# Passages between the parts of a float32 network on one core: program order written out, first products by token tile, norms on ScalarE and DVE

## The chip, the cores and the metric

The kernel runs on one core of a Trainium2 chip. TensorE (PE in the profile, its weight loads PEld) multiplies, VectorE (DVE), ScalarE (ACT) and GpSimd (POOL) do the rest, and SyncE (SP) issues the DMAs. The metric is the device time of one execution in microseconds; lower is better.

## The reference

Two blocks of a float32 network are applied to 256 tokens of 1024 channels. Each part adds its result to the residual x, and reads x through an RMS norm, `h = x * rsqrt(mean(x*x) + 1e-6) * g`, over the 1024 channels of a token:

```
x += (sigmoid(ga)*(attention @ w_a) + sigmoid(gb)*(gla @ w_b)) @ w_out     # mixer, 9 projections of h
a, u = split(h @ w_ffn_in); x += (silu(conv3(a)) * u) @ w_ffn_out          # FFN, 2816 wide
x += ((trailing_means(h) - h) @ w_pool per group of 256) * scale           # pool mixer
x += (silu(h @ w_gate) * (h @ w_up)) @ w_down                             # dense FFN, 2816 wide
x += ssd(h)                  # z, xbc, dt = h @ w_in; conv; chunked scan; gated norm; @ w_out
x += top 2 of 8 experts (3584 wide) by h @ w_router, weighted by their softmax
out = rmsnorm(x)
```

Each part needs the norm of the whole x of a token, that is the last sum of the part before it.

## The kernel before

**Tiles and stages.** The 256 tokens are two tiles of 128 on the partitions, t = 0 and 1; x stays in SBUF as two tiles of 128x1024, each in halves of 512 columns. The parts run one after the other (`network`, L1548). Every product of float32 matrices is made of three products of float32r parts, high by high, high by low and low by high (`mm3`, L337). Weights come by DMA on SP's queue into a ring of raw buffers (`fetch`, L287) of 128x2048; ScalarE copies the high part of each half of 1024 columns (`split`, L386: the copy is L391) and DVE subtracts it from the raw one to make the low part (L392). `piece` (L294) does that for one block of weights; there are six buffers for high halves (`wh`) and six for low halves (`wl`). In the experts the conversion is of 2048 columns at once (L311, L313).

**A norm** is `norm_tile` (L368): ScalarE squares both halves with a sum (L373), GpSimd multiplies the upper half by the gain (L374), DVE adds the two sums (L376), makes the reciprocal root by a shift, a constant and three rounds of tiny operations on 128x1 (`rsqrt`, L351 to L366), scales the lower half together with its gain (L378), and ScalarE scales the upper half (L379). Then `turn` (L398) transposes the tile's eight blocks by PE into two PSUM banks `tp` (L404) and splits them into the high and low part of xT (L391, L392). `Turned.tile` (L59) is the norm and the turn of one token tile.

**A passage** is what stands between the last products of one part and the first of the next: x of tile 0 is added (`add_x`, L429), normed and turned while tile 1's last products run, then the same of tile 1, then the first products of the next part for both tiles at once. There are three that the change touches: mixer to FFN (in `mixer`, L593), FFN through the pool mixer to the dense FFN (`down`, L778; `PoolMixer.tile`, L91), and dense FFN to SSD. In the pool mixer the trailing means are products with a band matrix, and the groups' outputs are products with w_pool. In both FFNs the first products are `sums` (L761): per block of 128 input channels and per bank, one matmul of 512 columns (both tiles, xT's high and low part by the high weights, L770) and one of 256 columns (L771); a chunk of weights is two banks of eight such pairs. In the SSD the first products are `z_chunk(0)` of 416 columns (`gemm_nat`, L409; `mm3`'s lines), for tile 0 and then for tile 1.

**What holds weights back and fills the waits.** After tile 1's turn `Turned.tile` sets `gates`: of the next pieces the first takes its low part on GpSimd, the next three wait with both their parts until the last split of xT has been issued (`piece`, L301 to L306). In the FFN and the dense FFN `keep_warm` (L328) puts 11 products whose results are not used ahead of tile 1's transposes; in the SSD none (the last argument of `Turned`, L1554 to L1556).

**Order.** The kernel is written with a planner that runs a timeline of its own when the program is built (`schedule_with_timeline_sim=True`, L1667) and fixes the order of the instructions on each engine: an operation that is ready by that timeline may be put ahead of one that stands earlier in the program. `issue_after` binds one instruction behind another. `in_order` (L1464) binds all instructions of PE, DVE and ACT issued from one point on in their program order, each engine for itself; others may still come between them. Before the change it is used in the experts. `Router` (L119) norms the input of the experts in its own way, with `rsqrt` in `scale` (L224).

## Time and profile before

| | |
|---|---|
| runs, us | 1767.45, 1766.4, 1769.3; median 1767.45 |
| the profiled execution, us | 1770.0; its span 1768.2 |
| PE busy | 1721.1 us, 97% of the span, 8731 matmuls |
| weight loads | 1420.7 us, 80% |
| DVE busy | 1495.5 us, 85%, 1652 instructions |
| ACT busy | 1245.7 us, 70%, 1412 instructions |
| GpSimd busy | 154.0 us, 9%, 118 instructions |
| DMA | 501.31 MB, mean 284 GB/s |
| chain that ended last | PE 55%, DVE 32%, issue 9% |

The span is the profiled execution on the core, from its first to its last recorded instruction. The granted clock of PE is given as a share of full speed, 2.4 GHz. A row of the timeline has the start, the duration, the engine, the line of the code, the operation, its result and its operands; in brackets is how long the engine was idle before it and what it waited for. Matmuls overlap their neighbours, so their pace is read from their starts. "x8" behind a row stands for eight instructions in a row.

### The profile page before, as it was taken

The numbers are of one execution on the slowest core, as the hardware profiler recorded it, in microseconds if no ns is written. First come the engines' busy times: TensorE is split into PE (matmuls) and PEld (weight loads), VectorE is DVE, ScalarE is ACT, GpSimd is POOL, SyncE is SP. The second block draws the span as 40 slices with busy tenths as digits, with TensorE's granted clock in tenths as the row PEclk, the third lists the DMA queues.
The fourth block names the chain that finished last, engine by engine and source line by source line (L and its number), as shares of the span: only waits on it lengthen the run. The fifth ranks groups of instructions, "written<-read, shape, count | busy, mean of one in ns | idle before, by whom it ended". The sixth has DMA issues, their size and how long they took to land.

```text
span 1768.2 us, 23830 instructions
## 1 busy us (share of the span) xinstructions
PE 1721.1 (97%) x8731; PEld 1420.7 (80%) x8731; DVE 1495.5 (85%) x1652; ACT 1245.7 (70%) x1412; POOL 154.0 (9%) x118
## 2 busy tenths in 40 slices
PE   8999989999999999999999999999999999999996
PEld 6878878888788879998878777777777787777775
DVE  7477668777766659997779999999999999999997
ACT  5564446655655546555468898888889888988895
POOL 1034010001100012572000000000000000000000
PEclk9999999999999999999989999999999999999999
DMA  8433455555455545425659999999999999999993
GB/s 288 167 120 123 143 183 211 185 188 188 143 188 188 188 150 204 143 97 179 253 187 373 420 421 421 420 418 420 405 402 420 421 420 415 421 420 410 421 420 157
DMA packets 72719, 501.31 MB, mean 284 GB/s; under 512 B 8322, under 2 KB 9346, under 8 KB 14355
## 3 DMA queue, kind: packets, MB, share of 16 engines
q1 hardware_dynamic: 72594, 499.71, 72.7%
q8 instruction: 71, 1.16, 0.3%
q14 instruction: 54, 0.43, 0.1%
HBM read 498.63 MB, written 1.05 MB: 283 GB/s over the span
## 4 chain that ended last, share of the span: by engine, by line
PE 55%; DVE 32%; issue 9%; ACT 2%; POOL 1%; DMA 0%; DVEq 0%; SPq 0%; ACTq 0%
DVE wl L313 23%; PE acc L339 7%; PE acc L340 7%; PE acc L341 7%; PE pr L770 5%; PE tp L770 5%; PE tp L771 2%; PE pr L771 2%; PE pr L339 2%; PE pr L340 2%; PE pr L341 2%; PE pr L1219 1%; PE pr L1218 1%; PE acc L516 1%; DVE wl L392 1%
## 5 line engine op out<-in xcount | busy, mean ns | idle before, releaser
L313 DVE TENSOR_TENSOR wl<-raw,wh 128x2048 fp32r<-128x2048 f32 x330 | 736.7, 2280 | 0.0
L311 ACT ACTIVATE wh<-raw 128x2048 fp32r<-128x2048 f32 x330 | 620.9, 1913 | 70.2 <-PE pr L341 38.8
L392 DVE TENSOR_TENSOR wl<-raw,wh 128x1024 fp32r<-128x1024 f32 (+2 forms) x248 | 308.2, 1255 | 112.7 <-ACT wh L391 109.8
L391 ACT ACTIVATE wh<-raw 128x1024 fp32r<-128x1024 f32 (+3 forms) x254 | 259.3, 1036 | 90.0 <-PE acc L341 60.1
L1219 PE MATMUL pr<-wl,xg 128*128 128x512 f32 x560 | 221.9, 396 | 5.5 <-DVE wl L313 5.5
L1218 PE MATMUL pr<-wh,xg 128*128 128x512 f32 x560 | 224.2, 400 | 0.0
L340 PE MATMUL pr<-wl,xg 128*128 128x512 f32 x336 | 135.8, 404 | 1.5 <-DVE wl L1462 1.5
L339 PE MATMUL pr<-wh,xg 128*128 128x512 f32 x336 | 136.6, 407 | 0.0
L341 PE MATMUL pr<-wh,xg 128*128 128x512 f32 x336 | 134.1, 399 | 0.0
L1219 PEld LDWEIGHTS pr<-wl,xg 128*128 128x128 f32 x560 | 105.3, 188 | 33.9 <-DVE wl L313 12.5
L770 PE MATMUL pr<-xT,wh 128*128 128x512 f32 x352 | 125.0, 398 | 2.0 <-DVE xT L392 2.0
L770 PE MATMUL tp<-xT,wh 128*128 128x512 f32 x352 | 124.9, 398 | 0.0
L1218 PEld LDWEIGHTS pr<-wh,xg 128*128 128x128 f32 x560 | 105.3, 188 | 22.2
L1219 PE MATMUL acc<-wl,hT 128*128 128x512 f32 x280 | 113.3, 405 | 1.6 <-DVE wl L313 0.4
L1218 PE MATMUL acc<-wh,hT 128*128 128x512 f32 x280 | 111.1, 397 | 0.7 <-DVE hT L392 0.7
L339 PE MATMUL acc<-wh,xT 128*128 128x512 f32 (+3 forms) x256 | 99.2, 389 | 1.6 <-ACT xT L391 0.9
L340 PE MATMUL acc<-wl,xT 128*128 128x512 f32 (+3 forms) x256 | 98.8, 387 | 0.0
L771 PE MATMUL tp<-xT,wl 128*128 128x256 f32 x352 | 98.6, 280 | 0.0
L771 PE MATMUL pr<-xT,wl 128*128 128x256 f32 x352 | 98.6, 280 | 0.0
L341 PE MATMUL acc<-wh,xT 128*128 128x512 f32 (+3 forms) x256 | 98.5, 387 | 0.1
L1536 POOL TENSOR_TENSOR raw<-x,raw 128x512 f32<-128x512 f32 x2 | 2.5, 1276 | 936.4 <-DVE x L431 936.4
L770 PEld LDWEIGHTS pr<-xT,wh 128*128 128x128 f32 x352 | 66.1, 188 | 18.4 <-DVE xT L392 2.4
(389 smaller groups left out, 3472.6 us busy)
## 6 DMA issues: line engine op xcount, KB each, us to landing
raw<-in_w_eg SPq DMA_DIRECT2D x110, 1024.0 KB, 10.6
raw<-in_w_ed SPq DMA_DIRECT2D x110, 1024.0 KB, 10.6
raw<-in_w_eu SPq DMA_DIRECT2D x110, 1024.0 KB, 10.8
raw<-in_w_ffn_in SPq DMA_DIRECT2D x22, 1024.0 KB, 4.9
raw<-in_w_dense_in SPq DMA_DIRECT2D x22, 1024.0 KB, 4.9
raw<-in_w_xbc SPq DMA_DIRECT2D x16, 1024.0 KB, 4.8
raw<-in_w_ffn_out SPq DMA_DIRECT2D x11, 1024.0 KB, 5.0
raw<-in_w_dense_out SPq DMA_DIRECT2D x11, 1024.0 KB, 4.9
```

The lines of the kernel that those rows point to most:

```text
L311: self.nc.scalar.activation(ab[0], raw, AF.Copy)
L313: lambda: v.tensor_tensor(ab[1], raw, ab[0].bitcast(F32), op=OP.subtract)
L339: mm(ps, st[0], mv[0], start=start, stop=False)
L340: mm(ps, st[0], mv[1], start=False, stop=False)
L341: self.last_mm = mm(ps, st[1], mv[0], start=False, stop=stop)
L391: a = nc.scalar.activation(h, src, AF.Copy)
L392: b = v.tensor_tensor(l, src, h.bitcast(F32), op=OP.subtract)
L516: nc.tensor.matmul(ps[:, m], wt.cut(a, k * 256 + m * P, P), xT[b][:, k], start=(k == 0 and a == 0 and b == 0), stop=(k == KB - 1 and b == 1))
L770: nc.tensor.matmul(ps, wh, xT[2][:, k], start=k == 0, stop=False)
L771: nc.tensor.matmul(ps[:, 0], wl, xT[0][:, k], start=False, stop=k == KB - 1)
L1218: self.nc.tensor.matmul(ps, st, mv[0], start=start, stop=False)
L1219: self.nc.tensor.matmul(ps, st, mv[1], start=False, stop=stop)
```

## The change

`Normed` replaces `norm_tile`. Its `half` squares one half of x on ScalarE, with a scale that makes the sum half of the mean, and multiplies the lower half by the gain on DVE; its `scale` makes the reciprocal root by `rsqrt_of` (the sum of both halves is taken in its first operation, and the constants differ), scales the lower half on ScalarE and the upper half with its gain on DVE. GpSimd has no part in it. The router's norm uses `rsqrt_of` too.

`Lead` holds the first weights of the next part: `fetch` reads them, `copy` and `subtract` make the parts of one half, `products` multiplies one half for one token tile. `LeadSums` does so for the first chunk of an FFN, with matmuls of 256 and 128 columns in place of 512 and 256, both banks of a tile for four blocks of channels at a time; `LeadRows` for the 416 columns of the SSD in four units, each per tile. `sums` and the SSD's first chunk use these results.

The instructions of each passage are issued in one written order, and `in_order` binds them: in the mixer from tile 0's last addition, ending with `both`; in the FFNs `down_last` takes the place of the last `down`: it fetches the next part's first weights, runs tile 0's last products, adds and norms tile 0, and within tile 1's last products calls `ready` (tile 0's turn, or its band products in the pool mixer, and the first weights' conversion), then `rest`. The pool mixer is cut into `means`, `split` and `mix` and its norm and that of the dense FFN are woven together. The `gates`, the products of `keep_warm` and GpSimd's low part of the first piece are gone.

```diff
+class Normed:
+    def __init__(self, net, g, xn):
+        self.net, self.g, self.xn = net, g, xn
+        self.ss = [net.small.tile([P, 2], F32, name="ss") for _ in range(2)]
+    def half(self, t, c):
+        net, nc, xn = self.net, self.net.nc, self.xn
+        h = slice(c * 512, (c + 1) * 512)
+        nc.scalar.activation(xn[:, t, 512:], net.x[:, t, h], AF.Square, scale=(0.5 / D) ** 0.5,
+                             accum_out=self.ss[t][:, c:c + 1])
+        if c == 0:
+            nc.vector.tensor_tensor(xn[:, t, h], net.x[:, t, h], self.g[:, h], op=OP.mult)
+    def scale(self, t):
+        net, nc, xn = self.net, self.net.nc, self.xn
+        r = net.rsqrt_of(self.ss[t], 1e-6)
+        nc.scalar.activation(xn[:, t, :512], xn[:, t, :512], AF.Copy, scale=r)
+        nc.vector.scalar_tensor_tensor(xn[:, t, 512:], net.x[:, t, 512:], r, self.g[:, 512:], op0=OP.mult, op1=OP.mult)
+class Turned(Normed):
+    def __init__(self, net, gname, lead=None):
+        super().__init__(net, net.gain(gname), net.norm.tile([P, 2, D], F32, name="xn"))
+        self.xT, self.lead = net.pair(KB), lead and lead(net)
+    def fetch(self):
+        self.lead.fetch()
+    def group(self, t, g, turned=None):
...
+        if turned is None:
+            turned = net.tp((P, 4, P))
+            for i in range(4):
+                nc.tensor.transpose(turned[:, i], self.xn[:, t, (4 * g + i) * P:(4 * g + i + 1) * P], net.ident)
+            return turned
+        last = net.split(turned, *[x[:, 4 * g:4 * g + 4, s] for x in self.xT[:2]])
+        if t == 0:
...
+    def turn(self, t):
+        for g in range(2):
+            self.group(t, g, self.group(t, g))
+    def ready(self):
+        self.turn(0)
+        self.lead.ready()
+    def rest(self):
+        lead, n = self.lead, self.lead.n
+        lead.subtract(n // 2)
+        self.scale(1)
+        for u in range(n // 2 + 1, n):
+            lead.subtract(u)
+        for u in range(n // 2 + 1):
+            lead.products(0, u, self.xT)
+        self.turn(1)
+        for u in range(n // 2 + 1, n):
+            lead.products(0, u, self.xT)
+        for u in range(n):
+            lead.products(1, u, self.xT)
+    def both(self):
+        ps = [self.group(0, g) for g in range(2)]
+        self.group(0, 0, ps[0])
+        net, s = self.net, slice(0, P)
+        net.nc.scalar.activation(self.xT[0][:, 4:, s], ps[1], AF.Copy)
+        self.scale(1)
+        self.early = net.nc.vector.tensor_tensor(self.xT[1][:, 4:, s], ps[1], self.xT[0][:, 4:, s].bitcast(F32), op=OP.subtract),
+        self.lead.products(0, 0, self.xT)
+        self.turn(1)
+        self.lead.products(0, 1, self.xT)
+        for h in range(2):
+            self.lead.products(1, h, self.xT)
+class Lead:
+    def __init__(self, net, aps, w):
+        self.net, self.aps, self.w = net, aps, w
+    def fetch(self):
+        raws = [self.net.fetch(ap, self.w) for ap in self.aps]
+        w = self.w // 2
+        self.raw = [raw[:, h * w:(h + 1) * w] for raw in raws for h in range(2)]
+        self.n, self.high, self.low = len(self.raw), {}, {}
+    def copy(self, u):
+        self.high[u] = self.net.whp.tile([P, 1024], F32R, name="wh")[:, :self.w // 2]
+        self.net.nc.scalar.activation(self.high[u], self.raw[u], AF.Copy)
+    def subtract(self, u):
+        self.low[u] = self.net.wlp.tile([P, 1024], F32R, name="wl")[:, :self.w // 2]
+        self.net.nc.vector.tensor_tensor(self.low[u], self.raw[u], self.high[u].bitcast(F32), op=OP.subtract)
+    def ready(self):
+        for u in range(self.n // 2):
+            self.copy(u)
+            self.subtract(u)
+        for u in range(self.n // 2, self.n):
+            self.copy(u)
+class LeadSums(Lead):
+    def products(self, t, h, xT):
+        net, mm = self.net, self.net.nc.tensor.matmul
+        if (t, h) == (0, 0):
+            self.ps = [net.pr((P, 2, T)) for _ in range(2)]
+        s = slice(t * P, (t + 1) * P)
+        for k in range(4 * h, 4 * h + 4):
+            for m in range(2):
+                c = slice(k % 4 * 256 + m * P, k % 4 * 256 + (m + 1) * P)
+                mm(self.ps[m][:, :, s], self.high[h][:, c], xT[2][:, k, :, s], start=k == 0, stop=False,
+                   skip_group_check=True)
+                mm(self.ps[m][:, 0, s], self.low[h][:, c], xT[0][:, k, s], start=False, stop=k == KB - 1,
+                   skip_group_check=True)
+class LeadRows(Lead):
+    def products(self, t, u, xT):
+        net, w = self.net, self.w // 4
+        if u == 0:
+            if t == 0:
+                self.ps = []
+            self.ps.append(net.acc())
+        s = slice(t * P, (t + 1) * P)
+        for i in range(2):
+            k, c = 2 * u + i, slice(i * w, (i + 1) * w)
+            net.mm3(self.ps[t][:, :w], (xT[0][:, k, s], xT[1][:, k, s]), (self.high[u][:, c], self.low[u][:, c]),
+                    k == 0, k == KB - 1)
+class PoolMixer(Normed):
...
+    def fetch(self):
+        self.N = self.then()
+        self.N.fetch()
+    def means(self, t, b, ps):
+        for g in range(2):
+            for i in range(4):
+                w, f = 2 * g + i // 2, slice((4 * g + i) * P, (4 * g + i + 1) * P)
+                c = slice(T, 3 * P) if b else slice(t * P, (t + 1) * P)
+                self.net.nc.tensor.matmul(ps[g][:, i], self.xn[:, b, f], self.band[:, w, c], start=b == 0 and i == 0,
+                                          stop=b == t and i == 3, skip_group_check=True)
...
+    def mix(self, t):
...
+        out = []
...
-            net.add_x(t, c, ps)
-        if t:
-            self.N.tile(1)
-            self.ctx.close()
+            out.append(ps)
+        return out
...
+    def ready(self):
+        ps = self.banks()
+        self.means(0, 0, ps)
+        self.split(0, ps)
+        self.N.lead.ready()
+    def rest(self):
+        net, N = self.net, self.N
+        N.lead.subtract(1)
+        self.scale(1)
+        out = self.mix(0)
+        ps = self.banks()
+        self.means(1, 0, ps)
+        for c in range(2):
+            net.add_x(0, c, out[c])
+            N.half(0, c)
+        self.means(1, 1, ps)
+        self.split(1, ps)
+        N.scale(0)
+        out = self.mix(1)
+        for c in range(2):
+            net.add_x(1, c, out[c])
+            N.half(1, c)
+        N.both()
+        self.ctx.close()
...
+        nc.scalar.activation(self.xh[:, t, h], x, AF.Square, scale=(0.5 / D) ** 0.5, accum_out=self.ss[:, t, c:c + 1])
...
+        self.r = net.rsqrt_of(self.ss[:, t], 1e-6)
...
-            gate = self.gates.pop(0) if self.gates else ()
...
+            fine = fine or self.wide is None
...
+    def rsqrt_of(self, ss, eps):
+        v = self.nc.vector
...
+        v.tensor_scalar(z, ss[:, 0:1], ss[:, 1:2], 0.5 * eps, op0=OP.add, op1=OP.add)
+        v.tensor_scalar(y.bitcast(I32), z.bitcast(I32), -0.5, float(0x5F3759DF - 0x400000 - 0x80000000), op0=OP.mult, op1=OP.add)
+        for _ in range(3):
+            v.tensor_scalar(t, y, y, z, op0=OP.mult, op1=OP.mult)
+            v.scalar_tensor_tensor(y, t, -1.5, y, op0=OP.add, op1=OP.mult)
+        return y
...
+            if then is not None and p == np_ - hold:
+                then.fetch()
+                for h in range(2):
+                    then.lead.copy(h)
+                    then.lead.subtract(h)
...
             def end(t, c, ps):
+                if (t, c) == (0, 1):
+                    self.start = len(nc.cur_bb.bb.instructions)
...
-                if c:
-                    N.tile(t)
-            for c in range(2):
-                self.gemm_nat(mT, I["w_out"][c], KB, end, c, last=True)
+                N.half(t, c)
+                if (t, c) == (0, 1):
+                    N.scale(0)
+            self.gemm_nat(mT, I["w_out"][0], KB, end, 0, last=True)
+            self.gemm_nat(mT, I["w_out"][1], KB, end, 1, last=True, then=N)
+            N.both()
+            self.in_order(self.start)
...
+        wt = None if lead else self.piece(ap)
...
+            ps = lead.ps[m] if lead else bank((P, 2, T))
+            for k in range(0 if lead else KB):
...
+    def down_last(self, aps, hT, accs, N):
+        wts = [self.piece(ap) for ap in aps]
+        N.fetch()
+        def sums(t, c, j):
+            for i in range(2):
+                h = hT[2 * j + i]
+                s = slice(t * P, (t + 1) * P)
+                self.mm3(accs[t][c], (h[0][:, s], h[1][:, s]), wts[j].both(i * 1024 + c * 512, 512), False,
+                         i == 1 and j == len(aps) - 1)
+        for j in range(len(aps)):
+            for c in range(2):
+                sums(0, c, j)
+        begin = len(self.nc.cur_bb.bb.instructions)
+        for c in range(2):
+            self.add_x(0, c, accs[0][c])
+            N.half(0, c)
+        N.scale(0)
+        for c in range(2):
+            for j in range(len(aps)):
+                if (c, j) == (1, 1):
+                    N.ready()
+                sums(1, c, j)
+            self.add_x(1, c, accs[1][c])
+            N.half(1, c)
+        N.rest()
+        self.in_order(begin)
...
+                a, u = self.sums(w_in[m], xT, self.tp if m % 2 else self.pr, pool, None if m else N.lead)
...
-            self.down([w_out[i + j] for j in range(3)], hs[2 * i:], accs, False, self.add_x, then=N)
+            self.down_last([w_out[i + j] for j in range(3)], hs[2 * i:], accs, N)
...
+                self.gemm_nat(xT, ap[max(c - 2, 0)], KB, gate_z, c, w=w, bank=bank)
...
-            z_chunk(0)
+            for t in range(2):
+                gate_z(t, 0, N.lead.ps[t][:, :416])
...
-            N.tile(t)
-        n.gates = []
-        N = n.mixer(N, lambda: Turned(n, "ln_ffn", 11))
-        M = n.ffn(N, I["w_ffn_in"], I["w_ffn_out"], True, lambda: PoolMixer(n, lambda: Turned(n, "dense", 11)))
-        N = n.ffn(M.N, I["w_dense_in"], I["w_dense_out"], False, lambda: Turned(n, "ssd", 0))
+            for c in range(2):
+                N.half(t, c)
+            N.scale(t)
+            N.turn(t)
+        sums = lambda w: lambda net: LeadSums(net, [w[0]], 2048)
+        N = n.mixer(N, lambda: Turned(n, "ln_ffn", sums(I["w_ffn_in"])))
+        M = n.ffn(N, I["w_ffn_in"], I["w_ffn_out"], True, lambda: PoolMixer(n, lambda: Turned(n, "dense", sums(I["w_dense_in"]))))
+        N = n.ffn(M.N, I["w_dense_in"], I["w_dense_out"], False,
+                  lambda: Turned(n, "ssd", lambda net: LeadRows(net, [I["w_z0"][0][0], I["w_z0"][0][1]], 1664)))
```

## Rows read from the trace of the kernel before

**Rows 1.** Windows: stretch, length, busy PE, PEld, DVE, ACT, POOL, clock, DMA, GB/s.
```profile
12.00:24.00 12.00, 10.34 (x41) 7.37 (x42) 11.60 (x23) 8.81 (x16) 3.83 (x2) 0.81 0.77 276
251.30:264.65 13.35, 10.65 (x60) 8.65 (x59) 10.89 (x20) 8.62 (x13) 1.28 (x1) 1.00 0.23 68
443.60:470.26 26.66, 22.96 (x156) 20.04 (x155) 21.39 (x48) 15.06 (x28) 6.44 (x5) 1.00 0.26 83
475.00:630.00 155.00, 155.00 (x829) 132.75 (x828) 99.67 (x138) 85.78 (x138) 0.00 (x0) 1.00 0.55 188
648.40:664.40 16.00, 13.49 (x67) 11.94 (x66) 11.53 (x20) 10.30 (x15) 3.09 (x2) 0.89 0.60 210
654.80:658.10 3.30, 3.30 (x12) 2.81 (x13) 1.38 (x2) 1.98 (x4) 0.00 (x0) 0.51 0.07 15
910.00:1700.00 790.00, 780.24 (x3490) 612.35 (x3490) 773.00 (x485) 685.31 (x523) 0.00 (x0) 1.00 1.01 413
```

**Rows 2.** Timeline of the first passage, all engines: start us, us, engine, line, operation.
```profile
251.31 1.03 PE L404 MATMUL tp<-ident,xn 128*128 128x128 f32 x8
251.51 0.69 DVE L431 TENSOR_TENSOR x<-x,acc 128x512 f32<-128x512 f32 x1 [0.69 <-PE acc L341]
...
252.44 0.62 ACT L373 ACTIVATE xn<-x 128x512 f32<-128x512 f32 x1
...
252.96 0.19 ACT L373 ACTIVATION_READ_ACCUMULATOR xn<-x 128x1 f32 x1
...
253.32 2.79 PE L335 MATMUL tp<-xT 128*128 128x512 f32 x11 [0.98 <-DVE xT L392]
...
258.15 1.29 DVE L392 TENSOR_TENSOR xT<-tp,xT 128x512 fp32r<-128x512 f32 x2 [1.44 <-ACT xT L391]
...
258.90 0.50 PE L770 MATMUL pr<-xT,wh 128*128 128x512 f32 x1 [0.98 <-DVE xT L392]
...
264.65 0.40 PE L770 MATMUL tp<-xT,wh 128*128 128x512 f32 x1
```

**Rows 3.** Timeline of PE in the second passage.
```profile
459.20 2.79 PE L335 MATMUL tp<-xT 128*128 128x512 f32 x11 [0.98 <-DVE xT L392]
...
470.26 0.39 PE L770 MATMUL tp<-xT,wh 128*128 128x512 f32 x1
```

**Rows 4.** Timeline of DVE at the start and before the first passage.
```profile
8.15 1.80 DVE L378 SCALAR_TENSOR_TENSOR xn<-x,rs_y,gbc 128x512 f32<-128x512 f32 x1 [1.07 <-DMA gbc<-in_gains]
...
16.16 0.14 DVE L376 TENSOR_TENSOR ss<-ss 128x1 f32<-128x1 f32 x1
...
17.06 1.22 DVE L392 TENSOR_TENSOR wl<-raw,wh 128x1024 fp32r<-128x1024 f32 x1
...
19.16 1.21 DVE L392 TENSOR_TENSOR wl<-raw,wh 128x1024 fp32r<-128x1024 f32 x1
...
21.29 0.75 DVE L378 SCALAR_TENSOR_TENSOR xn<-x,rs_y,gbc 128x512 f32<-128x512 f32 x1
...
247.61 0.54 DVE L376 TENSOR_TENSOR ss<-ss 128x1 f32<-128x1 f32 x1 [0.85 <-ACT xn L373]
...
250.07 0.75 DVE L378 SCALAR_TENSOR_TENSOR xn<-x,rs_y,gbc 128x512 f32<-128x512 f32 x1
```

**Rows 5.** Groups by line and shape, up to 920 us: busy us, mean ns | idle before, releaser.
```profile
L391 ACT ACTIVATE xT<-tp 128x512 fp32r<-128x512 f32 x20 | 11.5, 594 | 11.0 <-PE tp L404 11.0
...
L173 DVE TENSOR_TENSOR xs<-x,g 128x512 f32<-128x512 f32 x4 | 2.7, 688 | 0.0
```

**Rows 6.** Timeline of PE in the third passage.
```profile
654.79 1.90 PE L404 MATMUL tp<-ident,xn 128*128 128x128 f32 x8 [2.18 <-DVE xn L378]
...
664.20 0.35 PE L341 MATMUL acc<-wh,xT 128*128 128x416 f32 x1
664.39 0.28 PE L757 MATMUL acc<-xT,wl 128*128 128x256 f32 x1
664.51 0.28 PE L758 MATMUL acc<-xT,wh 128*128 128x256 f32 x1
```

More of the change, by code (lines that the diff above doesn't have):

```diff
@@ L47, in both @@
         return self.cut(0, a, w), self.cut(1, a, w)
-class Turned:
-    def __init__(self, net, gname, warm=0):
-        self.warm = warm
-        self.net, self.g = net, net.gain(gname)
-        self.xn = net.norm.tile([P, 2, D], F32, name="xn")
-        self.xT = net.pair(KB)
-    def tile(self, t):
-        self.net.norm_tile(t, self.g, self.xn)
-        if t and self.warm:
-            self.net.keep_warm(self.xT[0][:, 0, :P], self.xT[0][:, :4, :P], (self.net.turned, self.net.last_mm), self.warm)
-        last = self.net.turn(self.xn, KB, self.xT, ts=(t,))
-        if t:
-            self.net.gates = [(None,)] + [last] * 3
-        else:
-            self.early = last
@@ L73, in __init__ @@
     def __init__(self, net, then):
-        self.net, self.then, self.N = net, then, None
+        self.then, self.N = then, None
         I = net.I
@@ L81, in __init__ @@
         self.sc = net.gain("pool_scale", pool.tile([P, D], F32, name="sc"))
-        self.g = net.gain("pool", pool.tile([P, D], F32, name="g"))
-        self.xn = pool.tile([P, 2, D], F32, name="xn")
+        super().__init__(net, net.gain("pool", pool.tile([P, D], F32, name="g")), pool.tile([P, 2, D], F32, name="xn"))
         raw = net.fetch(I["w_pool"])
@@ L89, in __init__, with split @@
         self.wt = net.piece(Loaded(raw), pool=pool)
-    def tile(self, t):
-        net, nc, pT, xn, band = self.net, self.net.nc, self.pT, self.xn, self.band
-        net.norm_tile(t, self.g, xn)
-        s = slice(t * P, (t + 1) * P)
-        for g in range(0, 4, 2):
-            ps = net.tp((P, 4, P))
-            for i in range(4):
-                w, f = g + i // 2, slice((2 * g + i) * P, (2 * g + i + 1) * P)
-                nc.tensor.matmul(ps[:, i], xn[:, 0, f], band[:, w, s], start=True, stop=t == 0)
-                if t:
-                    nc.tensor.matmul(ps[:, i], xn[:, 1, f], band[:, w, T:], start=False, stop=True)
-            net.split(ps, pT[0][:, 2 * g:2 * g + 4, s], pT[1][:, 2 * g:2 * g + 4, s])
-        if t:
-            self.N = self.then()
-            self.N.tile(0)
+    def fetch(self):
[8 more added lines that the diff above has]
+                                          stop=b == t and i == 3, skip_group_check=True)
+    def split(self, t, ps):
+        s = slice(t * P, (t + 1) * P)
+        for g in range(2):
+            self.net.split(ps[g], *[p[:, 4 * g:4 * g + 4, s] for p in self.pT[:2]])
+    def mix(self, t):
+        net, pT = self.net, self.pT
+        s = slice(t * P, (t + 1) * P)
+        out = []
         for c in range(2):
@@ L249, in __init__ @@
         self.acts = pool("acts", 1)
[L250 removed]
+        self.ctx, self.rings, self.raws, self.nraw = ctx, rings, [], 0
         self.raw = self.more_raw(0, side="left")
@@ L407, in turn, with gemm_nat @@
         return last
-    def gemm_nat(self, xT, aps, kb, done, c, w=512, last=False, bank=None):
+    def gemm_nat(self, xT, aps, kb, done, c, w=512, last=False, bank=None, then=None):
         ps = [(bank or self.acc)() for _ in range(2)]
@@ L759, in pair_gemm, with sums @@
         return ps
-    def sums(self, ap, xT, bank, pool):
+    def sums(self, ap, xT, bank, pool, lead=None):
         nc = self.nc
-        wt = self.piece(ap)
+        wt = None if lead else self.piece(ap)
         out = []
         for m in range(2):
-            ps = bank((P, 2, T))
-            for k in range(KB):
+            ps = lead.ps[m] if lead else bank((P, 2, T))
+            for k in range(0 if lead else KB):
                 wh, wl = wt.both(k * 256 + m * P, P)
```

36 lines of the change are left out of this document (8 added, 28 removed).

## The prediction

> **What bounds the kernel now.** The stage windows come first. In the dense FFN the TensorE (PE) is busy for all 155.0 of 155.0 us; in the mixture of experts PE, DVE and DMA are all near full, the DMA at 413 GB/s [rows 1]. A stage of the first kind hands on an earlier or later start to the microsecond; the last one starts its stream of weights when its buffers come free, so it moves as a whole. What the change can win or lose is therefore what it wins or loses in the passages between parts, plus something at the start. The reader is to see in the windows how little that is. The first passage runs from PE's last product of w_out to the end of the first 256 columns of w_ffn_in, 251.30 to 264.65 us: 13.35 us, of which 2.70 idle and 2.79 filled by 11 warming products [rows 1, 2]. The second, FFN through pool mixer to dense FFN, 443.60 to 470.26, has 3.70 idle and the same filling again [rows 1, 3]. The third, dense FFN to SSD, 648.40 to about 664.3, has 2.51 idle and 3.30 us at a granted clock of 0.51, which is 1.2 of 2.4 GHz and costs 1.65 [rows 1]. Together 16 us lie open, 0.9% of the time.
>
> Then the timeline of one passage shows the order of waits: x is added (251.51), squared on ScalarE (252.44, readable at 253.15), a chain of tiny DVE operations makes the reciprocal root, xn is scaled, turned, copied, its low part taken, and PE starts at 258.90 [rows 2]. One norm chain undisturbed takes 2.46 us, of which 0.54 is the sum that the change drops [rows 4]; I take 1.95 for the new one and 0.72 for the scaling behind it (0.75 less what overlaps).
>
> **The change, part by part.** I lay the new program order out as one list per engine, each instruction starting when its engine and its inputs are there. Prices: adding x 0.66, a low part of xT 0.65 (two take 1.29), a Square readable 0.72 after it starts [rows 2]; a copy of xT 0.59 (0.5 where another follows), the product with the gain, now on DVE, 0.69 [rows 5]; a low part of 1024 weights 1.22 (1.18 in a row) [rows 4].
>
> *Split products.* A pair of matmuls of 512 and 256 columns costs 0.36 us now: 16 pairs fill 258.90 to 264.65 [rows 2]. By tiles it is 256 and 128 columns, twice. 256 columns follow each other at 0.12 [rows 6]; 128 columns I take at 0.11, as eight transposes of that width take 1.03 us with the drain of the last in it [rows 2] (bounds 0.06, half of 0.12, and 0.13, an eighth of 1.03). So 0.23 per pair and tile, 1.84 for half a chunk of one tile, 7.36 for all where 5.75 stood: 1.6 us more PE work in each of the first two passages.
>
> A rule of the skill speaks against this split. The Trainium skill, "TensorE: Matmul & The Clock Gate", section "LDWEIGHTS (loading the stationary operand)", gives a weight load as its columns over 1.2 GHz, 107 ns for 128, so that halving the moving columns below 256 saves hardly anything; the transposes agree with it. The same page's section "Back-to-back issue gap" has 81 ns per matmul sustained at 128 columns, by which a chunk would cost 6.4 us and the sum below would be 1.9 lower (an estimate); the transposes here are slower than that.
>
> *First passage.* DVE sets it. From 251.31: 0.2 to the end of the matmul, add 0.66, then 1.43 of waiting, since ScalarE's copy of xT now stands behind the Square (0.08+0.72+0.5+0.13), low part 0.65, norm 2.67, low part 0.65: 257.57. PE: the last four transposes to 258.09 (they waited for the PSUM bank of that low part), then three half chunks, 5.52: 263.61 against 264.65, so -1.0. The half that moved ahead is hidden by the norm of tile 1.
>
> *Second passage.* The band products of tile 0 go in among the last FFN products, which so end at 445.1 (16 passes of 0.11 later). From there, on DVE: wait 0.27, add 0.66, low weights 1.18, norm 2.67, add, gain, add 2.0, waiting behind two Squares 1.43, two low parts 1.3, norm 2.67, add, gain, add 2.0, waiting 1.43, low part 0.65, norm 2.67, low part 0.65. That is 19.6, so 464.7; PE +0.5 +5.5 gives 470.7 against 470.26 [rows 3]: +0.5. The early band products help nothing, because DVE is the chain and takes its operations in one fixed order.
>
> *Third passage.* Tile 0's turn goes in among tile 1's FFN products; its FFN products end at 640.1 (36 of 0.23 before the window's start) and its norm by the same list at 644.4. From there DVE has: add and gain 1.34, waiting 1.0, two low parts 1.3, two low parts of w_z0 1.96 (half of the four were GpSimd's; 1.2 by 832 of 1024 columns, 0.98 each), add 0.66, low weights 0.98, norm 2.67: 654.4. Tile 1's turn starts about where it does now, 654.79 [rows 6]. But then only the turn, 0.9, and five of eight units of 6 x 0.19 remain, 5.7: 661.1 against 664.3 [rows 6], -3.2.
>
> *The rest.* One DVE operation less in the router's chain: -0.2. At the start the scaling waits for the gain's DMA at 8.15 in either order [rows 4]; DVE takes over 0.69 per tile and loses contention and a tiny operation: 0, bounds -2 and +1. SP's queue keeps its order: gain and first weights of the next part are fetched into the same ring behind the same buffers. The removed GpSimd products lay off the path.
>
> At full clock and with nothing put between, the sum is -1.0+0.5-3.2-0.2 = -3.9.
>
> *Two costs on top.* (a) The clock. After 2.18 us without a product in the third passage the granted clock was 0.51 for 3.3 us [rows 1, 6]. My lists leave PE idle for 2.1 us in the first passage, 2.0 and 3.2 in the second, 1.7 in the third, the warming products being gone. A fall costs up to 1.65, less where PE waits anyway. I take 0.4, 0.6 and 0.7; bounds 0 and 5. (b) The gates that held back the weights of the next chunks are gone, and only the passage's own instructions are tied to each other. At the start, where no gates stood, two weight subtractions got into one chain: 5.13 us instead of 2.46 [rows 4]. Four such subtractions of 1.18 are ready in each of the first two passages (six buffers, raw weights there), two in the third. Each put in as soon as it is ready, they delay the three passages by 1.5, 3.5 and 2.4 in my lists: 7.4 at most, 0 at least. I take two that count, 2.4: the chains of this trace stand nearer to the clean end, the ungated one at the other.
>
> Sum: -3.9+1.7+2.4 = +0.2 on the profiled execution's 1770.0 (span 1768.2). That one lies 2.5 above the median of the runs, 1767.45; so 1767.7.
>
> **The rivals.**
> - *Weights get between* (slower). All ready subtractions go into the norm chains. Place: the norm of tile 1 in each passage, worst in the pool mixer, where DVE has no slack. Price: -3.9+1.7+7.4 = +5.2, 1772.7. It decides slower when more than 5.7 of the 7.4 are paid. For it: the start's chain. Against: DVE waits 1.43 three times, which swallows as many.
> - *Overlap as meant* (faster). Nothing gets between and the clock holds, as it does now over waits of about 1 us; the start gains a little, since GpSimd no longer slows DVE: a scaling took 1.80 beside GpSimd at 8.15 against 0.75 alone [rows 4], with DVE 97% busy and PE idle for 1.66 of 12 us there [rows 1]. -3.9-1 = -4.9: 1762.5. Against: the waits of 2 us above.
> - *No effect*: what it moves was hidden and the passages end where they did, 1767.5.
>
> On the second the Trainium skill, "SBUF — State Buffer", has the rule that a DVE operation with two SBUF inputs and a GpSimd one exclude each other on the shared port pair; the 1.80 agrees, and no number here hangs on it.
>
> **How the numbers follow.** A measurement of this kernel tells about 0.2%, 3.5 us, from no change. Forecast, some insertions and some falls of the clock: 0.45, own range 1764.5 to 1770.5. Overlap as meant: 0.27. Weights between: 0.25. No effect: 0.03. Nearly all of the overlap's lies beyond -3.5 (0.26) and most of the weights' beyond +3.5 (0.24), the rest within: 0.50. The hand-laid lists and the start are uncertain by 2.5 us together, so the range reaches that far past the two outer cases, 1762.5 and 1772.7: 1760 to 1775, one in ten left out on either side.
>
> **What would show it.** Right: the second passage no shorter than 26.7 us, counted from the last FFN product less the band products among them; the third about 3 shorter; a granted clock near 0.5 behind some of the idle stretches; weight subtractions of the next chunk between the tiny operations of a chain. Wrong: chains of 2 us with nothing between, a granted clock of 1.00 throughout, or a second passage below 26 us; then DVE is not its chain, and the change is faster than I say.

## The result, and the profile after

The changed kernel takes 1780.89 us (1780.25 to 1781.74), the kernel before in the same runs 1768.38: a ratio of 1.0071, 95% interval 1.0059 to 1.0084, so slower by 12.5 us. The forecast was 1767.7, the range 1760 to 1775. The profiled execution took 1780.25 us, its span is 10.2 longer than that of before; before's own execution lay 1.6 above its median and this one 0.6 below, which is the rest.

The head of the page, with the clock's row, of the kernel after:

```profile
span 1778.4 us, 23884 instructions
PE 1723.4 (97%) x8773; PEld 1427.7 (80%) x8773; DVE 1503.7 (85%) x1656; ACT 1246.9 (70%) x1412; POOL 127.1 (7%) x102
PEclk8999989999899999999989999999999999999999
```

Shares of busy time say nothing here: 97% as before. The clock's row has an 8 in the first, the sixth and the eleventh of the 40 slices, where before it has nines. The first is the start, where all kernels below but e3 have it; the others, 222 to 267 and 445 to 489 us, hold the first two passages. The windows of the kernel after (stretch, length, busy us of PE, PEld, DVE, ACT, POOL, clock, DMA share, GB/s) answer to [rows 1]: first the three passages, from the last product of the part before, then the stretches in them at half clock.

```profile
250.86:267.46 16.60, 12.55 (x83) 11.77 (x81) 9.63 (x22) 6.63 (x11) 0.00 (x0) 0.79 0.45 159
447.52:478.59 31.07, 23.75 (x163) 23.02 (x161) 22.23 (x47) 13.96 (x26) 0.00 (x0) 0.84 0.33 124
658.41:676.00 17.59, 13.12 (x65) 11.84 (x64) 13.11 (x22) 10.82 (x16) 0.00 (x0) 0.90 0.55 199
254.70:261.50 6.80, 6.05 (x28) 5.65 (x28) 4.03 (x12) 2.53 (x5) 0.00 (x0) 0.50 0.57 209
456.00:462.80 6.80, 5.85 (x27) 5.79 (x27) 4.77 (x11) 3.25 (x7) 0.00 (x0) 0.50 0.47 183
469.70:473.10 3.40, 3.40 (x19) 3.40 (x18) 2.04 (x7) 1.32 (x2) 0.00 (x0) 0.50 0.22 86
667.70:671.10 3.40, 3.40 (x14) 3.29 (x13) 3.40 (x5) 1.20 (x2) 0.00 (x0) 0.50 0.58 166
```

Where [rows 1] had the first passage at 13.35 us with 2.70 idle, it is now 16.60 with 4.05 idle and 6.8 us at half clock; the second had 26.66 with 3.70 idle, now 31.07 with 7.3 idle and 10.2 us at half clock. These windows begin at the start of the last product, 0.23 us earlier than those of [rows 1], and the second no longer holds tile 0's 16 band products, about 2 us, which now stand ahead of it.

Why PE idles stands in DVE's timeline (start, duration, engine, line, operation). In the first passage, the norm of tile 0, line by line from the first tiny operation to the scaling:

```profile
247.38 0.21 DVE L526 TENSOR_SCALAR rs_x<-ss 128x1 f32<-128x1 f32 x1 [0.85 <-ACT xn L60]
247.63 0.15 DVE L527 TENSOR_SCALAR rs_y<-rs_x 128x1 int32<-128x1 int32 x1
247.82 0.27 DVE L529 TENSOR_SCALAR rs_t<-rs_y,rs_x 128x1 f32<-128x1 f32 x1
248.13 0.16 DVE L530 SCALAR_TENSOR_TENSOR rs_y<-rs_t,rs_y 128x1 f32<-128x1 f32 x1
248.34 1.23 DVE L544 TENSOR_TENSOR wl<-raw,wh 128x1024 fp32r<-128x1024 f32 x1
249.48 0.27 DVE L529 TENSOR_SCALAR rs_t<-rs_y,rs_x 128x1 f32<-128x1 f32 x1
249.66 1.23 DVE L544 TENSOR_TENSOR wl<-raw,wh 128x1024 fp32r<-128x1024 f32 x1
250.81 0.15 DVE L530 SCALAR_TENSOR_TENSOR rs_y<-rs_t,rs_y 128x1 f32<-128x1 f32 x1
251.07 1.23 DVE L544 TENSOR_TENSOR wl<-raw,wh 128x1024 fp32r<-128x1024 f32 x1
252.21 0.27 DVE L529 TENSOR_SCALAR rs_t<-rs_y,rs_x 128x1 f32<-128x1 f32 x1
252.43 1.23 DVE L544 TENSOR_TENSOR wl<-raw,wh 128x1024 fp32r<-128x1024 f32 x1
253.58 0.15 DVE L530 SCALAR_TENSOR_TENSOR rs_y<-rs_t,rs_y 128x1 f32<-128x1 f32 x1
253.76 0.75 DVE L69 SCALAR_TENSOR_TENSOR xn<-x,rs_y,gbc 128x512 f32<-128x512 f32 x1
```

Four subtractions of the next chunks' weights stand one behind each of four tiny operations: the chain takes 6.38 us to the scaling, where tile 1's in the same trace takes 1.94 alone. The written order binds the chain's own operations to each other; the weights' are not among them.

In the second passage ScalarE is the first to be late. Its timeline, from the first weights' copies to tile 1's last Square:

```profile
445.69 2.00 ACT L149 ACTIVATE wh<-raw 128x1024 fp32r<-128x1024 f32 x2
447.58 3.88 ACT L543 ACTIVATE wh<-raw 128x1024 fp32r<-128x1024 f32 x4
451.37 0.61 ACT L60 ACTIVATE xn<-x 128x512 f32<-128x512 f32 x1
451.89 0.19 ACT L60 ACTIVATION_READ_ACCUMULATOR xn<-x 128x1 f32 x1
```

x was complete at 448.64 (the addition at 447.95 below); the Square waits for the last four of the six copies, those of the next chunks, and its sum is there at 452.08. DVE meanwhile takes the four subtractions and begins the norm when they are done, another 2.15 us later:

```profile
447.95 0.69 DVE L588 TENSOR_TENSOR x<-x,acc 128x512 f32<-128x512 f32 x1
...
449.69 4.62 DVE L544 TENSOR_TENSOR wl<-raw,wh 128x1024 fp32r<-128x1024 f32 x4
454.23 0.20 DVE L526 TENSOR_SCALAR rs_x<-ss 128x1 f32<-128x1 f32 x1
```

In the third passage ScalarE has the same, and a thing that I had not on my lists, the Exp of the SSD's decay (L1089) with its table load:

```profile
657.14 1.68 ACT L149 ACTIVATE wh<-raw 128x832 fp32r<-128x832 f32 x2
658.84 1.28 ACT L1089 ACT_TABLE_LOAD   x1
660.13 0.23 ACT L1089 ACTIVATE ea<-rows 128x32 f32<-128x32 f32 x1
660.27 1.67 ACT L149 ACTIVATE wh<-raw 128x832 fp32r<-128x832 f32 x2
661.85 1.99 ACT L543 ACTIVATE wh<-raw 128x1024 fp32r<-128x1024 f32 x2
663.74 0.61 ACT L60 ACTIVATE xn<-x 128x512 f32<-128x512 f32 x1
```

x was complete at 660.63, the Square starts at 663.74. Behind tile 1's scaling DVE then takes three subtractions of weights, two of them of the next chunks (667.10 to 670.30), before the low parts of xT.

To compare kernels whose order differs I take marks that stand behind each passage: the start of DVE's ninth `hl` subtraction of the FFN (319.15 us before) and of the dense FFN (524.04), from which on a kernel's distance to before stays the same through the rest of the FFN, the last product with w_xbc (788.66), the first of the experts (897.97), the end. Differences to the kernel before in each stretch between marks, in us, from the traces' timelines; the start is the first addition to x. "Chunk" is the distance from one `hl` subtraction to the next in the FFN and in the dense FFN, the last column the time at half clock in each of the three passages, by the records of the clock:

| kernel | start | 1st passage | 2nd | 3rd | router | experts | chunk, FFN and dense | half clock in 1st, 2nd, 3rd |
|---|---|---|---|---|---|---|---|---|
| before | | | | | | | 5.65, 5.55 | 0, 0, 3.4 |
| after | -0.2 | +2.3 | +7.0 | +2.0 | -1.2 | +0.2 | 5.55, 5.65 | 6.8, 10.2, 3.4 |
| e2 warm, no gates | +0.6 | +2.9 | +5.7 | +1.7 | -2.1 | -0.1 | 5.65, 5.65 | 3.4, 0, 0 |
| e3 before, no gates | +0.2 | +6.5 | +11.1 | +5.8 | -1.9 | -0.4 | 5.65, 5.65 | 6.8, 13.7, 6.8 |
| e4 before, no warm | -1.7 | +0.9 | +2.4 | 0.0 | -2.0 | -0.7 | 5.55, 5.55 | 6.8, 6.8, 3.4 |
| e5 gates, Exp misplaced | -0.2 | -0.5 | +6.0 | -2.5 | -0.2 | +0.1 | 5.65, 5.65 | 3.4, 10.2, 0 |
| e6 norms alone | -0.8 | -0.3 | -0.1 | -1.7 | -1.1 | 0.0 | 5.65, 5.65 | 0, 0, 0 |
| e7 gates, Exp | -2.0 | -1.1 | +3.4 | -2.5 | -1.9 | -0.4 | 5.55, 5.65 | 3.4, 6.8, 0 |
| e8 gates, Exp, warm | -1.6 | -1.9 | +0.5 | -2.6 | -1.2 | -0.4 | 5.55, 5.55 | 0, 0, 0 |
| e9 gates, planner's order | -1.1 | -1.8 | +2.4 | -1.2 | -1.2 | -0.1 | 5.65, 5.65 | 0, 6.8, 0 |
| e10 gates on DVE alone | +1.7 | -0.9 | +3.6 | +1.7 | -0.2 | -1.0 | 5.55, 5.55 | 3.4, 3.4, 6.8 |
| e11 Exp alone | +0.4 | +2.4 | +7.1 | +0.2 | -2.1 | -0.1 | 5.55, 5.65 | 6.8, 10.2, 0 |
| e12 no order, no gates | +0.6 | +2.8 | +3.1 | +2.9 | -1.2 | 0.0 | 5.55, 5.55 | 6.8, 3.4, 6.8 |

Two things limit what a row says. The chunks behind a passage follow at 5.55 or at 5.65 us, by the time of the mark a difference of 0.7, for a reason that I did not find; I name it where it counts, as "pace". And a trace is one execution: e4's took 3.4 us less than the median of its kernel, e10's 2.8 more, before's 1.6 to 2.7 more (by the set of runs), the others lie within 1.3. The start varies by 3.6 us between executions, the router's stretch by 2; the three passages are what differs by kernel.

### The profile page after: what moved, and what is told of

It reads as the page before. It is cut to its first block, busy times and chain, and to the rows that moved or that the text cites. A ratio compares the mean times of both kernels' runs of the same rounds, so it can differ in the third digit from the quotient of the medians.

```text
span 1778.4 us, 23884 instructions
## 1 busy us (share of the span) xinstructions
PE 1723.4 (97%) x8773; PEld 1427.7 (80%) x8773; DVE 1503.7 (85%) x1656; ACT 1246.9 (70%) x1412; POOL 127.1 (7%) x102
## 4 chain that ended last, share of the span: by engine, by line
PE 57%; DVE 30%; issue 9%; ACT 2%; POOL 1%; DMA 0%; DVEq 0%; SPq 0%; ACTq 0%
DVE wl L465 22%; PE acc L491 7%; PE acc L492 7%; PE acc L493 7%; PE tp L932 5%; PE pr L932 4%; PE tp L933 2%; PE pr L491 2%; PE pr L493 2%; PE pr L492 2%; PE pr L933 2%; PE pr L1412 2%; PE pr L1411 1%; PE acc L673 1%; DVE wl L544 1%
## 5 line engine op out<-in xcount | busy, mean ns | idle before, releaser
L543 ACT ACTIVATE wh<-raw 128x1024 fp32r<-128x1024 f32 (+2 forms) x246 | 252.5, 1038 | 87.8 <-PE acc L493 55.1
L1412 PEld LDWEIGHTS pr<-wl,xg 128*128 128x128 f32 x560 | 105.3, 188 | 34.3 <-DVE wl L465 12.9
L932 PE MATMUL pr<-xT,wh 128*128 128x512 f32 x320 | 113.5, 397 | 0.0
L933 PE MATMUL pr<-xT,wl 128*128 128x256 f32 x320 | 89.8, 281 | 0.0
L492 PEld LDWEIGHTS pr<-wl,xg 128*128 128x128 f32 x336 | 63.7, 190 | 19.6 <-DVE wl L465 3.8
L932 PEld LDWEIGHTS tp<-xT,wh 128*128 128x128 f32 x352 | 66.1, 188 | 16.0
## 6 DMA issues: line engine op xcount, KB each, us to landing
raw<-in_w_eg SPq DMA_DIRECT2D x110, 1024.0 KB, 10.2
```

Source lines behind the costliest of these rows:

```text
L492: mm(ps, st[0], mv[1], start=False, stop=False)
L543: a = nc.scalar.activation(h, src, AF.Copy)
L932: nc.tensor.matmul(ps, wh, xT[2][:, k], start=k == 0, stop=False)
L933: nc.tensor.matmul(ps[:, 0], wl, xT[0][:, k], start=False, stop=k == KB - 1)
L1412: self.nc.tensor.matmul(ps, st, mv[1], start=False, stop=stop)
```

## The experiments

Theories: **W**, conversions of the next chunks' weights get into the norm chains now that no gate holds them, and the clock falls because PE waits for those chains; **C**, the clock falls because the warming products are gone; **O**, the written order and the split products cost the time themselves. Medians in us; a ratio is to the kernel before in the same runs, with its interval.

**e1: the gates back.**

```diff
+        if self.lead is not None and t == 1 and g == 1:
+            net.gates = [last] * 3
...
+            for ins in self.gates.pop(0) if self.gates else ():
+                st.enter_context(self.tc.issue_after(ins.ins))
```

> The changed kernel (1780.9 us), with the six half conversions of the next three weight pieces held back until the last split of each passage. Theory W (weight conversions that are ready early are put into the norm chains; the idle PE and the fallen clock follow from that): the four subtractions of the first passage (5 us), the four copies and four subtractions of the second (about 5 us) and the two of the third leave the chains, and with them most of the 6.8 + 10.2 us at half clock: 1768 to 1773. Theory C (the clock falls because the warming products are gone, whatever stands in the chain): at most 3 us less, 1778 or more. Theory O (the written order and the products by tile cost the time themselves): no change, 1780 to 1781.

1770.34, ratio 1.0012 (1.0003 to 1.0021): 10.5 of the 12.5 us are gone. W, against C and O. No trace of it is shown; e7 has the same gates.

**e2: products in PE's waits, no gates.**

```diff
+        ps = self.net.acc() if n else None
+        for i in range(n):
+            self.net.nc.tensor.matmul(ps, self.high[0][:, :P], self.high[0][:, :512], start=True, stop=True)
```

> The changed kernel with products whose results are not used put in front of the operations for which PE waits longest: 12 in the first passage, 16 and 10 in the second, 14 in the third. The conversions stay in the chains. Theory W: the chains keep their length, only the half clock is won back where the work behind is PE's: 2 to 4 us less, 1777 to 1779. Theory C: the greater part comes back, 1773 or less. Theory O: no change.

1778.2, ratio 1.0057 (1.0044 to 1.0070): 2.7 less, as W had it. By the marks the second passage gains 1.3 and the first loses 0.6, which is the FFN's pace. Of 20.4 us at half clock in the passages 17 are gone, so with the conversions in the chains most of it must have stood where PE waits anyway.

**e3: the kernel before without its gates.**

```diff
-            self.net.gates = [(None,)] + [last] * 3
```

> The kernel before (1768.4 us) without the gates: no piece waits for the last split, and the first piece's low part is on DVE. Nothing else is changed. Theory W: conversions get into its chains as well, two to four a passage: 1771 to 1776. Theories C and O: no change to speak of, 1767 to 1770, since the warming products are still there and the order is the planner's.

1790.74, ratio 1.0123 (1.0108 to 1.0137): slower by 23, far more than any theory had. The direction settles that the gates, not the warming products, kept the chains clean; the size says that my prices for an insertion were low. DVE's timeline of it in the first passage shows tile 0's chain broken up in the same way, 8.18 us long where [rows 4] had 2.46:

```profile
247.80 0.54 DVE L376 TENSOR_TENSOR ss<-ss 128x1 f32<-128x1 f32 x1 [0.85 <-ACT xn L373]
...
251.67 1.22 DVE L392 TENSOR_TENSOR wl<-raw,wh 128x1024 fp32r<-128x1024 f32 x1
252.80 0.68 DVE L431 TENSOR_TENSOR x<-x,acc 128x512 f32<-128x512 f32 x1
253.40 0.27 DVE L361 TENSOR_SCALAR rs_t<-rs_y,rs_x 128x1 f32<-128x1 f32 x1
253.59 1.21 DVE L392 TENSOR_TENSOR wl<-raw,wh 128x1024 fp32r<-128x1024 f32 x1
...
255.98 0.75 DVE L378 SCALAR_TENSOR_TENSOR xn<-x,rs_y,gbc 128x512 f32<-128x512 f32 x1
```

Without gates the change is worth 10 us (1780.9 against 1790.7), with them it costs 2 (1770.3 against 1768.0).

**e4: the kernel before without its warming products.**

```diff
-        N = n.mixer(N, lambda: Turned(n, "ln_ffn", 11))
+        N = n.mixer(N, lambda: Turned(n, "ln_ffn", 0))
```

and the same for "dense".

> The kernel before without its two times 11 warming products; the gates stay. Theory W: PE idles 2.5 to 3.5 us in two passages, one or both clocks fall for 3.4 us: 1769 to 1772. Theory C: 1774 or more. Theory O: no change.

1772.44, ratio 1.0022 (1.0013 to 1.0031): 4.5 us by the medians, 3.9 by the ratio: just above W's range and below C's. Its windows of the first two passages:

```profile
249.56:264.60 15.04, 9.98 (x49) 8.48 (x48) 11.86 (x21) 8.84 (x13) 1.27 (x1) 0.77 0.25 90
442.80:471.84 29.04, 22.98 (x145) 20.36 (x144) 22.68 (x49) 15.25 (x28) 6.41 (x5) 0.88 0.30 100
```

A clock of 0.77 over 15.04 us and 0.88 over 29.04 is 2 x 0.23 x 15.04 = 6.9 and 7.0 us at half clock; by the marks the passages are 1.6 (0.9, and 0.7 of the FFN's pace taken off) and 2.4 longer, 0.3 of that time. Lost in full it would be half. The executions of the kernel before say the same: over the 87 recorded beside the experiments the time rises by 0.30 us per us at half clock (2 x (1 - granted clock) x span). That the rest stands where PE would wait anyway is argued, not shown.

**e5: gates, the Exp bound behind a DVE operation.**

```diff
-            with tc.issue_after(N.early[0].ins):
+            with tc.issue_after(N.late[1].ins):
```

> The kernel of e1 (1770.3), with the SSD's early Exp on ScalarE, which with its table load (1.5 us) stood between the copies of w_z0 in the third passage, put behind the last split of tile 1's turn. Theory S (ScalarE's queue, copies and Exp ahead of tile 1's last Square, makes that norm late): 1.0 to 1.7 us less, 1768.6 to 1769.3. Theory V (with the gates the chains are bound by DVE and PE alone): no change, 1770 to 1770.7. Its trace also shows how much of the first two passages' idle PE and half clock the gates leave: by theory W at most one fall in each; by theory C as many as in the changed kernel.

1772.1, ratio 1.0023 (1.0011 to 1.0036): not faster than e1 (1.8 more by the medians, inside the two intervals). ScalarE's timeline of it shows the Exp in the second passage, ahead of both Squares of tile 1:

```profile
459.47 1.28 ACT L1094 ACT_TABLE_LOAD   x1 [2.76 <-DMA rows<-in_rows]
460.76 0.23 ACT L1094 ACTIVATE ea<-rows 128x32 f32<-128x32 f32 x1
460.90 0.61 ACT L60 ACTIVATE xn<-x 128x512 f32<-128x512 f32 x1
```

An order bound behind another engine's instruction did not hold the Exp back on ScalarE; there it waited for its rows by DMA, and the Squares behind it. It says nothing on the place in the third passage, but it prices another: +2.5 us against e7 in the second passage, 3.4 us more at half clock among it.

**e6: the norms alone, in the kernel before** (the diff of `Normed` and `rsqrt_of`, put into `norm_tile`).

> The kernel before (1768.0) with the norms of the change alone (half mean from the Square's scale, one tiny operation less, the lower half's gain product on DVE, no GpSimd); order, gates and warming products as before. By the prediction's terms: 0.5 us less in each of the chains that set a passage (three to four) and 0.7 us more DVE work in some of them: 1765 to 1768.5. Rival: DVE, which is the chain, pays for the gain product in full each time: 1769 to 1771.

1766.35, ratio 0.9994 (0.9984 to 1.0004): within what was expected, not to be told from no change. By the marks the third passage gains 1.7, where before's trace has 3.4 us at half clock and this one none; so that may be the clock alone.

**e7: gates, the Exp bound behind ScalarE's own copy** (`N.late[0]` in the diff of e5).

> The kernel of e1 with the SSD's early Exp bound behind ScalarE's own copy of tile 1's last turned half. In e5 it was bound behind the DVE operation of that split, and the trace has it in the second passage (459.47 us), where it waited 2.76 us for its rows and loaded a table for 1.28 us. Theory S (ScalarE's queue): 1.0 to 1.7 us under e1's 1770.3, so 1768.6 to 1769.3. Theory V (no place of the Exp in the third passage counts): 1770 to 1771.

1765.94, ratio 0.9998 (0.9989 to 1.0008). Against e1 the ratio is 0.0014 lower, 2.5 us, between 0.2 and 4.8 by the two intervals: S rather than V, and more than S's 1.0 to 1.7 only within the noise. The third passage is 2.5 under before.

**e8: e7 with products in PE's waits** (8 ahead of tile 0's first products in two passages, 5 and 6 elsewhere; code as in e2).

> The kernel of e7 with products whose results are not used in PE's waits: 8 ahead of tile 0's first products in the first two passages, 5 ahead of the pool mixer's last band products, 6 ahead of tile 1's turn in the third. Theory W with the clock as its second part: the falls at 254.7 (3.4 us) and in the second passage are gone, 1.5 to 3 us under e7, 1766 to 1768. Rival: the products take as much as the clock gives back, 1768.5 to 1771.

1764.13, ratio 0.9982 (0.9972 to 0.9991): 0.2% faster than before, the best of all, and 1.8 under e7 by the medians, as W had it. Windows of the three passages, first of e7, then of e8:

```profile
249.34:262.36 13.02, 11.04 (x82) 10.61 (x80) 9.58 (x18) 8.35 (x12) 0.00 (x0) 0.87 0.20 52
442.50:469.89 27.39, 22.80 (x162) 21.90 (x161) 21.34 (x46) 13.82 (x26) 0.00 (x0) 0.88 0.22 72
650.20:668.00 17.80, 16.24 (x106) 15.48 (x106) 15.48 (x28) 14.51 (x22) 0.00 (x0) 1.00 0.77 280
```

```profile
249.68:261.86 12.18, 11.57 (x90) 10.53 (x88) 9.36 (x18) 8.33 (x12) 0.00 (x0) 1.00 0.18 52
441.30:467.15 25.85, 23.66 (x179) 21.62 (x177) 21.27 (x46) 14.46 (x26) 0.00 (x0) 1.00 0.24 73
647.00:665.00 18.00, 18.00 (x115) 17.04 (x116) 15.49 (x28) 14.70 (x23) 0.00 (x0) 1.00 0.78 287
```

The clock is 1.00 in all three of e8. DVE's chain in the first passage, tile 0, from its first tiny operation to the scaling with six others between:

```profile
245.98 0.21 DVE L541 TENSOR_SCALAR rs_x<-ss 128x1 f32<-128x1 f32 x1 [0.85 <-ACT xn L60]
...
247.93 0.75 DVE L69 SCALAR_TENSOR_TENSOR xn<-x,rs_y,gbc 128x512 f32<-128x512 f32 x1
```

1.95 us, nothing between.

**e9: gates, no written order.**

```diff
             N.both()
-            self.in_order(self.start)
```

and the same in `down_last`.

> The kernel of e1 without in_order in the three passages: the planner sets the order of PE, DVE and ScalarE, the gates stay. Theory O (the written order is what costs): 1768 or less. Theory W (it was the conversions, which the gates hold; the order neither costs nor gives more than 2 us): 1768.5 to 1772.5. A third way, the planner puts the first weights' own conversions into the chains: over 1773.

1766.62, ratio 0.9993 (0.9984 to 1.0003): as O had it. Against e1 the ratio is 0.0019 lower, 3.4 us, between 1 and 6: the written order costs something by itself, though the Exp stands ahead of tile 1's last Square here too. Part of it is the clock: over the whole span the median granted clock is 0.987 in e1 and 0.989 in e9, some 7 us less at half clock. Against e7 the times tell nothing; by the marks the first two passages are 1.5 (pace taken off) and 1.0 shorter, the third, with the Exp, 1.3 longer.

**e10: gates on DVE's subtractions alone.**

```diff
+            for ins in self.gates.pop(0)[1:] if self.gates else ():
```

(A gate is the pair of ScalarE's copy and DVE's subtraction of the last split; `[1:]` leaves the second.)

> The kernel of e7 (1765.9) with the gates on DVE's subtractions alone: ScalarE's copies of the next weights run as soon as they are ready, two or four of them (1 us each) ahead of a passage's last Square. Theory Q (the copies in ScalarE's queue delay a norm by themselves): 2 to 3 us more in the second passage, up to 2 in the third: 1768.5 to 1771. Theory D (only the subtractions in DVE's chains count; the Square waits for nothing that a copy delays): 1765 to 1767.5.

1771.96, ratio 1.0027 (1.0015 to 1.0039): above Q's span, 6.0 over e7 by the medians and 5.1 by the ratios. By the marks it is the third passage, +4.2 against e7, and hardly the second (+0.9, pace taken off). ScalarE's timeline of it there:

```profile
652.32 3.25 ACT L152 ACTIVATE wh<-raw 128x832 fp32r<-128x832 f32 x4
655.47 2.00 ACT L548 ACTIVATE wh<-raw 128x1024 fp32r<-128x1024 f32 x2
657.37 0.62 ACT L60 ACTIVATE xn<-x 128x512 f32<-128x512 f32 x1
```

x was complete at 655.81, so the two copies hold the Square for 1.6 us; behind it 6.8 us stand at half clock (660.1 to 666.9), where e7 has none in this passage. e11 has the same two copies there, no half clock in its trace, and +0.2 against before where e10 has +1.7. So copies alone make a norm late, by 1.6; the rest of the 4.2 goes with the clock that fell behind it. By the ratios they cost about half of what copies and subtractions cost together (e1).

**e11: the Exp alone moved, no gates** (`N.late[0]`).

> The changed kernel (1780.9) without gates, with the SSD's early Exp bound behind ScalarE's copy of tile 1's last turned half. If the Exp with its table load is paid in full in the third passage: 1.5 to 2 us less, 1779 to 1779.5. If the free copies of weights take its place in ScalarE's queue: 1780 to 1781.5.

1778.1, ratio 1.0058 (1.0038 to 1.0078): 2.8 less by the medians, but the two intervals overlap, so it is the trace that tells. Tile 1's norm begins 2.31 us after x is complete (661.40), in the changed kernel 3.85 (660.63 to 664.48):

```profile
663.71 0.21 DVE L527 TENSOR_SCALAR rs_x<-ss 128x1 f32<-128x1 f32 x1 [1.37 <-ACT xn L60]
```

The 1.54 between is the load and the Exp: paid in full. By the marks the third passage is 1.9 shorter, and the 3.4 us at half clock in it are gone as well.

**e12: no written order, no gates** (the diff of e9 in the changed kernel).

> The changed kernel without in_order and without gates: the fourth corner beside the changed kernel (order, no gates, 1780.9), e1 (order, gates, 1770.3) and e9 (gates, no order, 1766.6). If the written order costs by itself what e9 gained on e1: 3 to 4 us less, 1777 to 1778. If the written order also keeps some conversions out of the chains when no gate does (the kernel before, in the planner's order and without gates, paid 23 us in e3): 1784 to 1792. If it does neither: 1780 to 1782.

1777.69, ratio 1.0058 (1.0041 to 1.0075): 3.2 less than with the order by the medians, 2.3 by the ratios, between -1.4 and 6.0: nearest to the first case and against the second, but not clear of no change. By the marks the second passage is 3.9 shorter (0.7 of it pace), the others 0.5 and 0.8 longer. With e1 and e9 the four corners are 1780.9, 1770.3, 1777.7, 1766.6: the missing gates cost 10.6 and 11.1 in either order, the written order 3.2 and 3.7, the first of these uncertain.

## Why the prediction was wrong

*The sum at full clock with nothing between held.* It gave -1.0, +0.5 and -3.2 for the passages; e8, where the gates keep the chains clean, the Exp is out of the way and the clock is 1.00, has -1.2 (pace taken off), +0.5 and -2.6. Its whole gain, 3.2 us, is near the -3.9. For the third passage forecast and measurement both count from a trace with 3.4 us at half clock there, so part of that gain is the clock's (at most the 1.7 of e6). One sum is 0.3 short, which changes nothing: 16 passes of 0.11 behind 443.60 end at 445.4, not at 445.1. The price of split products, 0.23 us per pair and tile, held too: 24 pairs from 261.87 to 267.46 in the kernel after, 0.233 each. By the Trainium skill, "TensorE: Matmul & The Clock Gate", section "LDWEIGHTS (loading the stationary operand)", two loads of 107 ns make an estimated 0.214; the trace lies 9% above that. With the same page's 81 ns per matmul (section "Back-to-back issue gap") and 0.12 for the 256 columns the pair would be 0.20, an estimate too, and the trace is 16% above it.

*The step that failed is "Two costs on top"*, 1.7 + 2.4 where some 15 stood. From the marks: after less e8 is 4.2 + 6.6 + 4.6 = 15.4 us in the three passages. Of it

- 1.9 is the Exp with its table load in ScalarE's queue (e11), which my lists did not have, and the 3.4 us at half clock that went with it;
- 3.1 is what clock was left to fall once the chains were clean (e7 to e8, 10.2 us at half clock), and 0.7 the dense FFN's pace;
- 9.6 is the conversions between and the clock that fell for them (after to e11 to e7). Half-clock time fell by 3.4 + 3.4 us in the first two passages from e11 to e7; at the 0.3 of e4 and of e7 to e8 that is an estimated 2.0, and leaves 7.6 for the conversions proper.

So the insertions came out at about their upper bound, 7.4, where I took 2.4, and the clock at an estimated 6 where I took 1.7 and allowed 5. The split depends on what is taken away first: with the conversions still between, the clock was worth 2.7 (e2). "I take two that count" leaned on the clean chains of a trace whose gates were there to keep them clean; the one ungated chain in it, at the start [rows 4], was the right row. And the two costs were taken as separate, though each insertion lengthens the wait in which the clock falls: 6.8 and 10.2 us at half clock where 3.4 a fall had been read.

*The right rival was too cheap.* "Weights get between" had the mechanism and the sign, with 0.25 and 1772.7. Its place was only half right: in the first passage the four go into tile 0's chain, which I held to be hidden beside w_out's last products and which stops being so at 6.38 us; and in two passages ScalarE's copies, which I had not listed, make a Square late, though in the second DVE's subtractions end 2.15 us after its sum is there.

*What would show it:* the half clock and the weights between tiny operations are there; the second passage is no shorter than 26.7 us (31.07). The third, which should have been 3 shorter, is 2 longer.

*The small terms.* The router's stretch is 1.2 shorter, but varies by 2. At the start DVE's first scaling, beside which no GpSimd product runs now, takes 0.75 us (at 9.03) where it took 1.80 [rows 4]; whether the start is shorter for it cannot be told from its own spread.

*The written order* had a price too that my lists did not show: some 3 us (e9, between 1 and 6; e12 alone would not tell), by the marks in the first two passages with gates and in the second without. The lists themselves were laid in that order, and e8 meets them; what they lack is the better order that the planner finds. That the lists are right step by step is not shown, only that their sums are.

Open: what in the first two passages the planner does better; why the kernel before pays 23 us for its missing gates and the changed one only 11; and why the chunks have two paces.

## What to carry to other kernels

Before taking out an ordering constraint, list what it holds back, on every engine that this work runs on, and price all of it in the worst place: what is ready gets in. An order written for a chain does not keep others out of it; only a bound on the others does. Where TensorE's wait grows, price the clock with it, not beside it.

## What the runs showed of the hardware

Half-clock time cost 0.3 of its length where PE partly waited (e4: 13.9 us cost 4.0; e7 to e8: 10.2 us cost 3.1; 0.30 over 87 executions of the kernel before), and less where long chains held PE up anyway (e2: 17 us less brought 2.7). Products whose results are not used, put in PE's waits, held the clock at 1.00 in all three passages (e8). A table load of 1.28 us and its Exp on ScalarE, far from any product, made a norm 1.54 us late and moved the end of its passage by 1.9 (e11).
